# Token-major blocks of 1024 columns, with transposed MLP activations, in a two-layer encoder trunk

## The chip, the cores and the metric

The kernel runs on one core of a Trainium2 chip. What counts is the time of one launch on the device, in microseconds (us); of several runs the median is taken. One further execution of each kernel is recorded by the hardware profiler, and the views of the profile that are read below come from it.

## What is computed

256 tokens of width 2048 go through two layers, in float32. Each layer has a mixer and an MLP, each between two norms. What matters here is the size of the products: the weights of the whole trunk are read once, and everything else is small beside them.

```python
D_MODEL, SEQ, DEPTH, D_FF = 2048, 256, 2, 8192
def reference(x, norm_g, even_w_in, ..., mlp_w1, mlp_w2):
    h = x
    for l in range(DEPTH):
        g = norm_g[l]
        u = rmsnorm(h, g[0])
        if l % 2 == 0:
            proj = u @ even_w_in[e]                      # 2048 x 6144
            b_gate, c_gate, hc, q, k, v = split_cols(proj, EVEN_SIZES)
            ya = short_conv_mixer(b_gate, c_gate, hc, even_conv_w[e])
            yb = chunked_band_attention(q, k, v, even_rel_bias[e])
            y = jnp.concatenate([ya, yb], axis=-1) @ even_w_out[e]     # 2048 x 2048
        else:
            proj = u @ odd_w_in[o_i]                     # 2048 x 7184
            hq, hf, hi, hg, gq, gk, gv, gr, ga = split_cols(proj, ODD_SIZES)
            yc = hgrn2_mixer(hq, hf, hi, hg, lb_all[l], hgrn_norm_g[o_i])
            yd = gla_mixer(gq, gk, gv, gr, ga, gla_wa2[o_i], gla_ba[o_i], gla_norm_g[o_i])
            y = jnp.concatenate([yc, yd], axis=-1) @ odd_w_out[o_i]    # 2048 x 2048
        h = h + rmsnorm(y, g[1])
        u = rmsnorm(h, g[2])
        z = jnp.square(jax.nn.relu(u @ mlp_w1[l])) @ mlp_w2[l]         # 2048 x 8192, 8192 x 2048
        h = h + rmsnorm(z, g[3])
    return h
```

## The kernel before

**Number format.** Each float32 operand is split into a high and a low part of the type fp32r, and each product is made of three: high by high, high by low, low by high.

**Slabs.** Weights come in slabs of 512 KB: one DMA on SyncE's queue into `raw` (3 buffers), a cast on ScalarE to `whi` (L226), and a subtraction on VectorE to `wlo` (L227); `whi` and `wlo` have 8 buffers each, so casts can run ahead of TensorE. There are 784 such loads. Two forms of block use them:

- `Block` is token-major: the activations are the stationary operand, 128 tokens at a time (tile t = 0, then t = 1), and the weights stream by. A slab holds two k-tiles (2 x 128 rows) of 512 columns; for each token tile it gives six matmuls of 512 columns (L240 high by high, L241 by the weights' low part, L242 the activations' low part), 12 a slab. All six add to one PSUM bank (`acc`), which is evacuated after the block's last slab.
- `UpBlock` is feature-major: 128 columns of the weights are stationary, and the activations of all 256 tokens, high and low beside one another, stream by. A slab gives eight pairs of one matmul of 512 columns (L275) and one of 256 (L276), in four banks. The product comes out transposed, as the next product needs it.

Eight PSUM banks are divided: `acc` has `ACC_BUFS` = 3, `aux` has `AUX_BUFS` = 5 (transposes, the small products, and the four banks of the MLP's UpBlocks; `banks()` gives the even mixer two of each).

**Stages.** The even mixer (q, k and the convolution as UpBlock, 80 slabs; v as Block, 16), its output projection `out_proj` (4 Blocks of 8 slabs), the MLP `mlp`, then the odd mixer (112 slabs: `hgrn` twice with f, q, i, g, then `gla` with k, q, r, v, all Block), its `out_proj` and the second MLP. An MLP has 8 chunks of 1024 hidden columns. `up(c)` makes two blocks of 512 columns (8 slabs each), UpBlock but for the very first of each layer, which is a Block whose squares are transposed on TensorE; `down(c-1)` follows `up(c)`, with 4 Blocks of 4 slabs whose results are added into `y` on VectorE (L473). In the odd mixer and the output projection's input, operands that are token-major are turned by `transpose4` (four 128 x 128 transposes on TensorE, L185, into one `aux` bank) and split by `split4` (a copy on ScalarE, a subtraction on VectorE).

**Order.** `run` writes out slabs one after another: load, then the matmuls of both token tiles. With `lead`, the first 6 slabs (`LEAD`) do tile 0 first and tile 1 after; with `tail`, the last 4 slabs (`TAIL`) do so, and `between` puts the norm of tile 0 ahead of the matmuls of tile 1. `later` delays what needs TensorE (transposes) by two slabs; `bg` holds small work of the mixers as generators, a step of which is taken every 1 / `rate` slabs. From this the framework's scheduler sets the order of each engine when the kernel is built, and each engine then runs its own in order.

**Names.** `xt` are the normed activations, `x2` the second product's, `relu`, `relu2`, `ulo` the hidden values on the way. In the odd mixer, `ev_f` turns the forget gate into its logarithm (L871 to L874 on ScalarE), which is then transposed.

```python
            for i in range(SLAB):
                xh, xl = self.lhs(t, self.kts[s * SLAB + i])
                ...
                nc.tensor.matmul(ps, xh, hi[:, i, 0:self.n], start=first, stop=False)
                nc.tensor.matmul(ps, xh, lo[:, i, 0:self.n], start=False, stop=False)
                nc.tensor.matmul(ps, xl, hi[:, i, 0:self.n], start=False, stop=last)
```

## Time and profile before

| what | value |
|---|---|
| runs | 2306.0, 2307.85, 2311.98 us; median 2307.85 |
| span of the profiled execution | 2302.9 us |
| TensorE matmul, busy (PE) | 2276.5 us |
| TensorE weight load, busy (PEld) | 1920.3 us |
| VectorE busy (DVE) | 1412.6 us |
| ScalarE busy (ACT) | 1093.6 us |
| GpSimd busy (POOL) | 15.3 us |
| DMA, mean | 186 GB/s |

The span is that of the program on the core; the runs are launches and lie 3.1 to 9.1 us above it. Times of instructions below are counted from the span's start. A row of the timeline gives start, duration, engine, line and operation, the output and the inputs by their names, and in brackets the idle time ahead of it on its engine and what ended that. A matmul's duration overlaps with that of its neighbours, so that two starts, not one duration, give what it costs.

### The profile page before, as it was taken

What the parts mean: (1) busy time and instruction counts of PE and PEld (TensorE: products, weight loads), DVE (VectorE), ACT (ScalarE), POOL (GpSimd) and SP (SyncE); (2) the same over time, 40 slices, a digit from 0 to 9 for tenths busy, and PEclk for the clock granted to TensorE, in tenths of its full rate; (3) what the DMA queues carried; (4) which work ended last, traced back from release to release, by engine and by line L of the source; (5) the groups of instructions that cost most, each with busy time, mean ns of one, the idle gap of its engine ahead of it and who ended that gap; (6) DMA issues with size and microseconds to landing.
All of it is one profiled execution on the core that took longest, in us unless ns stands there. A gap on an engine that the chain in (4) does not pass through costs nothing.

```text
span 2302.9 us, 30049 instructions
## 1 busy us (share of the span) xinstructions
PE 2276.5 (99%) x11518; PEld 1920.3 (83%) x11518; DVE 1412.6 (61%) x1873; ACT 1093.6 (47%) x1565; POOL 15.3 (1%) x30
## 2 busy tenths in 40 slices
PE   9999999999999999999999999999999999999998
PEld 7888888888888888888788888888888888888886
DVE  6656565755555555555777767657656555555555
ACT  6444445544444444444646454546444444444443
POOL 0000000000000000000000000000000000000000
PEclk9999999999999999999999999999999999999999
DMA  7564665655655556555554544565665655655653
GB/s 242 183 187 150 192 205 172 212 189 192 191 186 190 192 187 189 191 190 193 181 193 156 165 146 156 171 243 167 209 193 189 191 190 186 192 192 185 191 192 119
DMA packets 219231, 428.35 MB, mean 186 GB/s; under 512 B 13362, under 2 KB 14160, under 8 KB 218832
## 3 DMA queue, kind: packets, MB, share of 16 engines
q1 hardware_dynamic: 216992, 420.53, 56.2%
q0 software_dynamic: 1376, 4.79, 0.7%
q8 instruction: 90, 1.47, 0.2%
q10 hardware_dynamic: 720, 1.11, 0.1%
q14 instruction: 53, 0.43, 0.1%
HBM read 422.18 MB, written 4.20 MB: 185 GB/s over the span
## 4 chain that ended last, share of the span: by engine, by line
PE 87%; DMA 5%; DVE 4%; ACT 3%; issue 1%; DVEq 0%; ACTq 0%; POOLq 0%; SPq 0%
PE aux L275 20%; PE acc L240 17%; PE acc L242 17%; PE acc L241 17%; PE aux L276 10%; DMA raw<-e_win 2%; DVE wlo L227 2%; DMA raw<-w 2%; PE acc L275 2%; ACT whi L226 2%; PE aux L796 1%; PE aux L185 1%; PE acc L276 1%; ACT xt L176 1%; ACT junk L359 0%
## 5 line engine op out<-in xcount | busy, mean ns | idle before, releaser
L227 DVE TENSOR_TENSOR wlo<-raw,whi 128x1024 fp32r<-128x1024 f32 x780 | 953.7, 1224 | 785.2 <-ACT whi L226 783.5
L226 ACT CAST whi<-raw 128x1024 fp32r<-128x1024 f32 x780 | 821.5, 1054 | 1038.0 <-PE acc L242 509.8
L275 PE MATMUL aux<-xt,whi 128*128 128x512 f32 x2240 | 798.2, 398 | 1.5 <-DVE relu L453 1.5
L276 PE MATMUL aux<-xt,wlo 128*128 128x256 f32 x2240 | 628.4, 281 | 0.0
L275 PEld LDWEIGHTS aux<-xt,whi 128*128 128x128 f32 x2240 | 421.0, 188 | 105.8 <-DVE relu L453 2.1
L240 PE MATMUL acc<-whi,x 128*128 128x512 f32 x1264 | 493.2, 390 | 1.1 <-DVE relu L476 0.7
L242 PE MATMUL acc<-whi,x 128*128 128x512 f32 x1264 | 492.3, 389 | 0.0
L241 PE MATMUL acc<-wlo,x 128*128 128x512 f32 x1264 | 492.2, 389 | 0.0
L276 PEld LDWEIGHTS aux<-xt,wlo 128*128 128x128 f32 x2240 | 423.1, 189 | 0.5
L240 PEld LDWEIGHTS acc<-whi,x 128*128 128x128 f32 x1264 | 237.3, 188 | 51.0 <-DVE relu L476 1.1
L242 PEld LDWEIGHTS acc<-whi,x 128*128 128x128 f32 x1264 | 237.3, 188 | 49.8
L241 PEld LDWEIGHTS acc<-wlo,x 128*128 128x128 f32 x1264 | 237.3, 188 | 48.7
L240 PE MATMUL acc<-whi,xt 128*128 128x512 f32 x576 | 229.5, 399 | 0.3 <-ACT gate L882 0.3
L241 PE MATMUL acc<-wlo,xt 128*128 128x512 f32 x576 | 226.5, 393 | 0.0
L242 PE MATMUL acc<-whi,xt 128*128 128x512 f32 x576 | 226.0, 393 | 0.0
L242 PEld LDWEIGHTS acc<-whi,xt 128*128 128x128 f32 x576 | 108.7, 189 | 23.2 <-issue 0.3
L240 PEld LDWEIGHTS acc<-whi,xt 128*128 128x128 f32 x576 | 108.8, 189 | 22.4 <-ACT gate L882 0.7
L241 PEld LDWEIGHTS acc<-wlo,xt 128*128 128x128 f32 x576 | 108.9, 189 | 21.4
L275 PE MATMUL acc<-xt,whi 128*128 128x512 f32 x320 | 121.9, 403 | 3.8 <-DVE whole L619 3.8
L276 PE MATMUL acc<-xt,wlo 128*128 128x256 f32 x320 | 90.5, 283 | 0.0
L275 PEld LDWEIGHTS acc<-xt,whi 128*128 128x128 f32 x320 | 60.6, 189 | 18.8 <-DVE whole L619 4.4
L473 DVE TENSOR_TENSOR y<-acc,y 128x512 f32<-128x512 f32 x96 | 61.5, 682 | 0.0
(208 smaller groups left out, 1103.6 us busy)
## 6 DMA issues: line engine op xcount, KB each, us to landing
raw<-w SPq DMA_DIRECT2D x512, 512.0 KB, 3.6
raw<-o_win SPq DMA_DIRECT2D x112, 512.0 KB, 3.7
raw<-e_win SPq DMA_DIRECT2D x96, 512.0 KB, 4.2
raw<-e_wout SPq DMA_DIRECT2D x32, 512.0 KB, 4.3
raw<-o_wout SPq DMA_DIRECT2D x32, 512.0 KB, 3.9
gbc<-norm_g SPq DMA_DIRECT2D x8, 512.0 KB, 6.0
h<-x SPq DMA_DIRECT2D x8, 256.0 KB, 5.4
hsave<-h POOLq DMA_DIRECT2D x2, 1024.0 KB, 4.7
```

The lines of the kernel that those rows point to most:

```text
L176: nc.scalar.activation(out=hi[:, k, :], in_=psv[:, k, :], func=AF.Copy, scale=g[:, k:k + 1])
L185: nc.tensor.transpose(out=ps[:, k * P:(k + 1) * P], in_=src[:, k * P:(k + 1) * P], identity=ident)
L226: nc.scalar.copy(out=hi[:, :, 0:self.n], in_=raw[:, :, 0:self.n])
L227: nc.vector.tensor_tensor(out=lo[:, :, 0:self.n], in0=raw[:, :, 0:self.n], in1=hi[:, :, 0:self.n], op=ALU.subtract)
L240: nc.tensor.matmul(ps, xh, hi[:, i, 0:self.n], start=first, stop=False)
L241: nc.tensor.matmul(ps, xh, lo[:, i, 0:self.n], start=False, stop=False)
L242: nc.tensor.matmul(ps, xl, hi[:, i, 0:self.n], start=False, stop=last)
L275: nc.tensor.matmul(self.ps[j], hi[:, i, cs], x, start=first, stop=False)
L276: nc.tensor.matmul(self.ps[j][:, 0:NT * P], lo[:, i, cs], x[:, 0, :], start=False, stop=last)
L473: nc.vector.tensor_tensor(out=y[t][:, cs], in0=ps, in1=y[t][:, cs], op=ALU.add)
L796: nc.tensor.matmul(ps[0:m, u * 64:(u + 1) * 64].rearrange("p (b n) -> p b n", n=wd), K[:, u * P:u * P + m], Q[:, us].rearrange("p (b two n ...
```

## The change

A third form of block comes in, `Wide`: token-major like Block, but a slab holds one k-tile of 1024 columns, where Block's holds two k-tiles of 512. It is 512 KB as well and gives 12 matmuls of 512 columns too. The two column halves go to two `acc` banks, written in turn, so that one stationary operand serves up to four matmuls after one another. The two halves needn't be neighbours in the weights (`step`). A block has as many slabs as k-tiles, twice as many as a Block over the same rows, and two evacuations for each token tile.

Wide takes the place of Block in both output projections, in the MLP's `down` and in the odd mixer, where f and q, i and g, k and q, the two halves of r and of v are paired; GLA's `decay` now stands ahead of the block for k and q instead of behind that for k. In the MLP, Wide also takes the place of UpBlock in `up`: one block of 16 slabs a chunk. The hidden values then come out token-major: ScalarE takes the ReLU, VectorE the square into `ulo` (now 4 buffers), and two slabs later `transpose4` and `split4` turn them, four sets of four transposes a chunk, into `aux` banks. `acc` gets five banks, `aux` three; the even mixer's UpBlocks, which stay, take three `acc` banks and one `aux`. The even mixer's v stays Block. Of the 784 slabs 688 are now Wide, 80 UpBlock and 16 Block; the loads are as many and as large as before.

```diff
-ACC_BUFS = 3
-AUX_BUFS = 5
+ACC_BUFS = 5
+AUX_BUFS = 3
...
+    class Wide(Block):
+        def __init__(self, wv, n0, n1, kts, lhs, evac):
+            super().__init__(wv, n0, 512, kts, lhs, evac)
+            self.step = n1 - n0
+            self.nslab = len(kts)
+
+        def source(self, s):
+            k = self.kts[s]
+            if self.step == 512:
+                return self.wv[:, k:k + 1, self.n0:self.n0 + 1024].rearrange("p a (b n) -> p (a b) n", n=512)
+            a = self.wv[:, k, self.n0:self.n0 + 512]
+            return bass.AP(tensor=a.tensor, offset=a.offset, ap=[a.ap[0], [self.step, 2], [1, 512]])
+
+        def mm(self, s, t):
+            if s == 0:
+                self.ps[t] = [accp.tile([P, 512], F32, name="acc") for _ in range(2)]
+            ps = self.ps[t]
+            hi, lo = self.w[s]
+            xh, xl = self.lhs(t, self.kts[s])
+            first, last = s == 0, s == self.nslab - 1
+            nc.tensor.matmul(ps[0], xh, hi[:, 0, :], start=first, stop=False)
+            nc.tensor.matmul(ps[1], xh, hi[:, 1, :], start=first, stop=False)
+            nc.tensor.matmul(ps[0], xh, lo[:, 0, :], start=False, stop=False)
+            nc.tensor.matmul(ps[1], xh, lo[:, 1, :], start=False, stop=False)
+            nc.tensor.matmul(ps[0], xl, hi[:, 0, :], start=False, stop=last)
+            nc.tensor.matmul(ps[1], xl, hi[:, 1, :], start=False, stop=last)
+            if last:
+                for j, e in enumerate(self.evac):
+                    e(t, ps[j])
+                del self.ps[t]
...
     def banks():
-        return [accp.tile([P, 512], F32, name="acc") if j % 2 == 0 else aux() for j in range(4)]
+        return [accp.tile([P, 512], F32, name="acc") if j < 3 else aux() for j in range(4)]
...
-        run([Block(wview(w), nb * 512, 512, kts if nb == 0 else ALLK, X2.get, mk(nb)) for nb in range(4)],
-            tail=TAIL, between=between, extra=ypool, hooks=hooks)
+        run([Wide(wview(w), nb * 512, nb * 512 + 512, kts if nb == 0 else ALLK, X2.get, [mk(nb), mk(nb + 1)])
+             for nb in (0, 2)], tail=TAIL, between=between, extra=ypool, hooks=hooks)
...
-                    r2 = ypool.tile([P, 512], F32, name="ulo", bufs=2)
+                    r2 = ypool.tile([P, 512], F32, name="ulo", bufs=4)
                     nc.vector.tensor_tensor(out=r2, in0=r, in1=r, op=ALU.mult)
-                    later(lambda: hid[c].put(t, c * 2 + j, split4(x2p, "x2", transpose4(r2, accp, "acc"))))
+                    later(lambda: hid[c].put(t, c * 2 + j, split4(x2p, "x2", transpose4(r2))))
                 return evac
-            def mk_up(j):
...
-            return [Block(w1v, (c * 2 + j) * 512, 512, ALLK, X.get, mk(j)) if c == 0 and j == 0 else
-                    UpBlock(w1v, (c * 2 + j) * 512, 512, ALLK, X.both, mk_up(j)) for j in range(2)]
+            return [Wide(w1v, c * 1024, c * 1024 + 512, ALLK, X.get, [mk(0), mk(1)])]
...
-            return [Block(w2v, nb * 512, 512, list(range(c * 8, c * 8 + 8)), hid[c].get, mk(nb)) for nb in range(4)]
+            return [Wide(w2v, nb * 512, nb * 512 + 512, list(range(c * 8, c * 8 + 8)), hid[c].get, [mk(nb), mk(nb + 1)])
+                    for nb in (0, 2)]
...
-        return [Block(wv, HF + g * 512, 512, ALLK, X.get, ev_f),
-                Block(wv, HQ + g * 512, 512, ALLK, X.get, ev_q),
-                Block(wv, HI + g * 512, 512, ALLK, X.get, ev_i),
-                Block(wv, HG + g * 512, 512, ALLK, X.get, ev_g)]
+        return [Wide(wv, HF + g * 512, HQ + g * 512, ALLK, X.get, [ev_f, ev_q]),
+                Wide(wv, HI + g * 512, HG + g * 512, ALLK, X.get, [ev_i, ev_g])]
...
-        return ([Block(wv, GK, 512, ALLK, X.get, ev_k)], decay,
-                [Block(wv, GQ, 512, ALLK, X.get, ev_q)] +
-                [Block(wv, GR + i * 512, 512, ALLK, X.get, mk_r(i)) for i in range(2)] +
-                [Block(wv, GV + i * 512, 512, ALLK, X.get, mk_v(i)) for i in range(2)])
+        return decay, [Wide(wv, GK, GQ, ALLK, X.get, [ev_k, ev_q]),
+                       Wide(wv, GR, GR + 512, ALLK, X.get, [mk_r(0), mk_r(1)]),
+                       Wide(wv, GV, GV + 512, ALLK, X.get, [mk_v(0), mk_v(1)])]
...
-    first, decay, rest = gla()
-    run(first, rate=RATE)
+    decay, blocks = gla()
     decay()
-    run(rest, rate=RATE)
+    run(blocks, rate=RATE)
```

How this moves instructions on the engines is shown at the places of which the prediction speaks. Rows give line, operation, output and inputs (names with the number of the buffer) and the shape.

**From up to down in the MLP.** TensorE before: the end of an up block (UpBlock, `aux` banks) and the start of the down blocks:

```order
L275 MATMUL aux_6387<-xt_3501,whi_6538 128x512
L276 MATMUL aux_6387<-xt_3501,wlo_6539 128x256
L240 MATMUL acc_6588<-whi_6584,x2_5643 128x512
L241 MATMUL acc_6588<-wlo_6585,x2_5643 128x512
L242 MATMUL acc_6588<-whi_6584,x2_5643 128x512
L240 MATMUL acc_6588<-whi_6584,x2_5643 128x512
```

The down block takes an `acc` bank that stood idle, and no transposes stand between. TensorE in the changed kernel at the same place, from the last two matmuls of the up block (`acc_5306` and `acc_5307`, the banks of its second token tile) on:

```order
L275 MATMUL acc_5306<-whi_5568,xt_3498 128x512
L276 MATMUL acc_5307<-whi_5568,xt_3498 128x512
L271 MATMUL acc_5606<-whi_5602,x2_4983 128x512
L272 MATMUL acc_5607<-whi_5602,x2_4983 128x512
L273 MATMUL acc_5606<-wlo_5603,x2_4983 128x512
L274 MATMUL acc_5607<-wlo_5603,x2_4983 128x512
L275 MATMUL acc_5606<-whi_5602,x2_4983 128x512
L276 MATMUL acc_5607<-whi_5602,x2_4983 128x512
L271 MATMUL acc_5614<-whi_5602,x2_4999 128x512
L273 MATMUL acc_5614<-wlo_5603,x2_4999 128x512
L272 MATMUL acc_5615<-whi_5602,x2_4999 128x512
L274 MATMUL acc_5615<-wlo_5603,x2_4999 128x512
```

The down block's first slab asks for four banks within twelve matmuls: one stands idle (`acc_5606`), the others are those of the ended block, in the order in which they are read. TensorE in the changed kernel right behind that slab:

```order
L185 MATMUL aux_5622<-ident_82,ulo_5580 128x128 x4
L185 MATMUL aux_5630<-ident_82,ulo_5584 128x128 x4
L185 MATMUL aux_5638<-ident_82,ulo_5594 128x128 x4
L271 MATMUL acc_5606<-whi_5656,x2_4983 128x512
L272 MATMUL acc_5607<-whi_5656,x2_4983 128x512
L273 MATMUL acc_5606<-wlo_5657,x2_4983 128x512
L274 MATMUL acc_5607<-wlo_5657,x2_4983 128x512
L275 MATMUL acc_5606<-whi_5656,x2_4983 128x512
L276 MATMUL acc_5607<-whi_5656,x2_4983 128x512
L271 MATMUL acc_5614<-whi_5656,x2_4999 128x512
L272 MATMUL acc_5615<-whi_5656,x2_4999 128x512
L185 MATMUL aux_5646<-ident_82,ulo_5598 128x128 x4
```

Twelve transposes of the hidden values (`ulo`) now stand behind the down block's first slab, and the last four come eight matmuls later.

ScalarE before, at the end of an up block (the copies of the half products, L449, the casts of weights, L226, and the splits, L458):

```order
L449 COPY ulo_7970<-aux_7808 128x256
L449 COPY ulo_7978<-aux_7809 128x256
L449 COPY ulo_7990<-aux_7810 128x256
L226 CAST whi_8140<-raw_8138 128x1024
L449 COPY ulo_7998<-aux_7811 128x256
L458 CAST x2_7983<-relu2_7981 128x512
L226 CAST whi_8160<-raw_8158 128x1024
L458 CAST x2_8003<-relu2_8001 128x512
```

ScalarE in the changed kernel, around the end of an up block (casts of weights, L229, the four ReLUs, L474, the split, L172):

```order
L229 CAST whi_5746<-raw_5744 128x1024
L474 ACTIVATE relu_5578<-acc_5298 128x512
L474 ACTIVATE relu_5582<-acc_5299 128x512
L229 CAST whi_5764<-raw_5762 128x1024
L474 ACTIVATE relu_5592<-acc_5306 128x512
L474 ACTIVATE relu_5596<-acc_5307 128x512
L229 CAST whi_5786<-raw_5784 128x1024
L172 CAST x2_5627<-aux_5622 128x512
L172 CAST x2_5635<-aux_5630 128x512
```

Four reads of 256 columns, each ahead of VectorE's add, have become four ReLUs of 512 columns, two for each token tile, with a cast of weights between the two pairs.

**The forget gate in the odd mixer.** TensorE before, where the gate's block (`hgrn`, f) has ended and its neighbour has begun:

```order
L240 MATMUL acc_9742<-whi_9792,xt_9372 128x512
L241 MATMUL acc_9742<-wlo_9793,xt_9372 128x512
L242 MATMUL acc_9742<-whi_9792,xt_9372 128x512
L240 MATMUL acc_9742<-whi_9792,xt_9372 128x512
L185 MATMUL aux_9756<-ident_82,v_9708 128x128 x4
L241 MATMUL acc_9742<-wlo_9793,xt_9372 128x512
```

The transposes of the gate (`v_9708`) stand within a slab whose weights are already cast. ScalarE before, at the gate's evacuation (L871) and its logarithm (L873, L874):

```order
L226 CAST whi_9810<-raw_9808 128x1024
L871 ACTIVATE tmp_9709<-acc_9574,nrst_9553 128x512
L226 CAST whi_9828<-raw_9826 128x1024
L873 ACTIVATE tmp_9710<-tmp_9709 128x512
L871 ACTIVATE tmp_9726<-acc_9581,nrst_9557 128x512
L874 ACTIVATE tmp_9710<-tmp_9710 128x512
```

ScalarE in the changed kernel at the end of the paired block of f and q (L889 reads f's bank, L900 q's, L891 and L892 are the logarithm):

```order
L229 CAST whi_9502<-raw_9500 128x1024
L229 CAST whi_9533<-raw_9531 128x1024
L229 CAST whi_9551<-raw_9549 128x1024
L229 CAST whi_9569<-raw_9567 128x1024
L889 ACTIVATE tmp_9345<-acc_9064,nrst_9043 128x512
L900 ACTIVATE gate_9355<-acc_9065,rs_o_8907 128x512
L891 ACTIVATE tmp_9346<-tmp_9345 128x512
L889 ACTIVATE tmp_9357<-gate_9355 128x512
L892 ACTIVATE tmp_9346<-tmp_9346 128x512
```

The gate's evacuation now comes 16 slabs into the mixer instead of 8, behind the cast of slab 22, where the block ends with slab 15; both banks are read there.

**The end of the program.** VectorE before, the last column block of the second token tile and the norm:

```order
L476 TENSOR_TENSOR relu_19203<-acc_19178,y1_12668 128x512
L480 SCALAR_TENSOR_TENSOR y1_12668<-relu_19203,pw2_13548,gbc_13377 128x512
L128 TENSOR_SCALAR rs_v_19208<-ssl_13381,pw4b_13551,based_19102 128x1
L134 SCALAR_TENSOR_TENSOR rs_a_19213<-rs_r_19210,rs_v_19208 128x1
L139 SCALAR_TENSOR_TENSOR rs_o_19215<-rs_a_19213,rs_r_19210 128x1
L579 SCALAR_TENSOR_TENSOR h1_12663<-y1_12668,rs_o_19215,h1_12663 128x256
```

VectorE in the changed kernel:

```order
L493 TENSOR_TENSOR relu_18172<-acc_18003,y1_12158 128x512
L493 TENSOR_TENSOR relu_18183<-acc_18004,y1_12158 128x512
L497 SCALAR_TENSOR_TENSOR y1_12158<-relu_18172,pw2_13039,gbc_12867 128x512
L161 TENSOR_REDUCE rs_t_18177<-ssy_12869 128x1
L497 SCALAR_TENSOR_TENSOR y1_12158<-relu_18183,pw2_13039,gbc_12867 128x512
L155 TENSOR_SCALAR basec_18179<-rs_t_18177,pw4a_13041 128x1
L156 TENSOR_SCALAR based_18180<-basec_18179 128x1
L128 TENSOR_SCALAR rs_v_18188<-ssl_12871,pw4b_13042,based_18180 128x1
L134 SCALAR_TENSOR_TENSOR rs_a_18193<-rs_r_18190,rs_v_18188 128x1
L139 SCALAR_TENSOR_TENSOR rs_o_18195<-rs_a_18193,rs_r_18190 128x1
L597 SCALAR_TENSOR_TENSOR h1_12153<-y1_12158,rs_o_18195,h1_12153 128x256
```

Two column blocks (L493, L497) instead of one stand here, and the sum of the partial squares (L161 to L156) comes between them.

**The start.** TensorE before, in the first slabs, which both programs have as Blocks of the even mixer's v:

```order
L242 MATMUL acc_153<-whi_253,xt_262 128x512
L241 MATMUL acc_160<-wlo_254,xt_262 128x512
L240 MATMUL acc_153<-whi_299,xt_262 128x512
L242 MATMUL acc_160<-whi_253,xt_262 128x512
L240 MATMUL acc_160<-whi_253,xt_262 128x512
L241 MATMUL acc_160<-wlo_254,xt_262 128x512
```

The scheduler mixes the matmuls of the two token tiles, so that two banks are written in turn; in the changed kernel the rows are the same but for the line numbers.

26 lines of the change are left out of this document (6 added, 20 removed).

## The prediction

> **What bounds the kernel now.** I read the page first, then the chain, then the timeline of TensorE at one chunk of the MLP and at every place where it paused.
>
> ```profile
> PE 2276.5 (99%) x11518; PEld 1920.3 (83%) x11518; DVE 1412.6 (61%) x1873; ACT 1093.6 (47%) x1565; POOL 15.3 (1%) x30
> PE 87%; DMA 5%; DVE 4%; ACT 3%; issue 1%; DVEq 0%; ACTq 0%; POOLq 0%; SPq 0%
> ```
>
> TensorE is busy for 99% of the span, and 87% of the chain that ended last is its own. So a time comes out of three things: how many matmuls there are, at what pitch they start, and where TensorE waits. A matmul's duration is not its pitch, since they overlap; pitches are read from starts. One chunk of the MLP in the steady state (16 slabs of UpBlock, then 16 slabs of Block):
>
> ```profile
> 711.28 0.39 PE L275 MATMUL aux<-xt,whi 128*128 128x512 f32 x1
> ...
> 756.50 0.40 PE L240 MATMUL acc<-whi,x 128*128 128x512 f32 x1
> ...
> 800.08 0.39 PE L275 MATMUL aux<-xt,whi 128*128 128x512 f32 x1
> ```
>
> ```profile
> 711.28:756.50 45.22, 45.22 (x258) 39.24 (x257) 24.79 (x28) 19.79 (x25) 0.00 (x0) 1.00 0.57 187
> 756.50:800.08 43.58, 43.58 (x195) 36.03 (x193) 26.73 (x30) 18.55 (x20) 0.00 (x0) 1.00 0.60 193
> ```
>
> In the window rows the columns after the length are busy PE, PEld, DVE, ACT and POOL, then clock, DMA share and GB/s. Both halves do the same multiplications, 16 slabs each, yet the feature-major half takes 45.22 us and the token-major half 43.58 us: 2.826 against 2.724 us a slab, and 43.58 / 192 = 0.227 us a matmul. TensorE never pauses there; VectorE (24.8 of 45.2) and ScalarE (19.8) have room.
>
> **The change, part by part.** *Pitch.* 30 of the MLP's 32 up blocks, 8 slabs each, turn from UpBlock into token-major slabs. 240 slabs x (2.826 - 2.724) = 24.6 us less. This takes the pitch of Block for that of Wide, whose consecutive matmuls write two banks in turn and keep one stationary operand for four. Both occur already: at the start the scheduler mixes the two token tiles, so that from 24.42 on acc_160, acc_153, acc_160 are written one after the other (the rows in the order shown above):
>
> ```profile
> 24.42 0.39 PE L241 MATMUL acc<-wlo,xt 128*128 128x512 f32 x1
> 24.65 0.39 PE L240 MATMUL acc<-whi,xt 128*128 128x512 f32 x1
> 24.88 0.39 PE L242 MATMUL acc<-whi,xt 128*128 128x512 f32 x1
> 25.11 0.39 PE L240 MATMUL acc<-whi,xt 128*128 128x512 f32 x1
> 25.33 0.39 PE L241 MATMUL acc<-wlo,xt 128*128 128x512 f32 x1
> ```
>
> Pitch 0.23, 0.23, 0.23, 0.22: no other than in Block. L240 to L241 keeps the stationary operand, L241 to L242 doesn't, at the same pitch. So I take 0.227 for Wide; the stages that were Block already gain and lose nothing.
>
> *Transposes.* The activations now pass through TensorE: 16 transposes a chunk (twelve, then four in the order), 16 chunks, where two blocks had eight each. Their price is read from two places of the odd mixer:
>
> ```profile
> 1257.71 0.40 PE L242 MATMUL acc<-whi,xt 128*128 128x512 f32 x1
> 1257.94 0.60 PE L185 MATMUL aux<-ident,tmp 128*128 128x128 f32 x4
> 1258.30 0.47 PE L240 MATMUL acc<-whi,xt 128*128 128x512 f32 x1
> ...
> 1259.77 0.40 PE L240 MATMUL acc<-whi,xt 128*128 128x512 f32 x1
> ...
> 1386.80 0.39 PE L242 MATMUL acc<-whi,xt 128*128 128x512 f32 x1
> 1387.03 1.03 PE L185 MATMUL aux<-ident,tmp 128*128 128x128 f32 x8
> ...
> 1389.29 0.39 PE L240 MATMUL acc<-whi,xt 128*128 128x512 f32 x1
> ```
>
> From 1257.71 to 1259.77 are 2.06 us with seven pitches of 0.227 in them, so four transposes add 0.47; from 1386.80 to 1389.29 are 2.49 us, so eight add 0.90. That is 0.108 each and 0.04 for the interruption. Twelve and four: 0.04 + 12 x 0.108 + 0.47 = 1.80 us a chunk, 28.8 for 16, less 2 x 0.90 before: 27.0 us more. Pitch and transposes together: +2.4 us, nearly nothing.
>
> The evacuations: 4 copies and adds of 256 columns a block, then squares and splits, become 2 ReLUs, 2 squares and 2 splits of 512. They go beside TensorE in both programs, and the window rows leave 20 us of VectorE free in each half; I cost them at nothing but for one wait.
>
> *Banks.* A Wide block ends four banks where Block ended two, and five buffers hold accumulators. At the end of an up block ScalarE reads all four, and the order has a cast of weights between the second ReLU and the third. Nearest rows:
>
> ```profile
> L471 ACT COPY y<-acc 128x512 f32<-128x512 f32 x16 | 9.4, 589 | 8.6 <-PE acc L242 8.6
> L226 ACT CAST whi<-raw 128x1024 fp32r<-128x1024 f32 x780 | 821.5, 1054 | 1038.0 <-PE acc L242 509.8 <-PE aux L275 369.9 <-DMA raw<-e_win 43.9
> ```
>
> ```profile
> 2293.53 0.39 PE L242 MATMUL acc<-whi,x 128*128 128x512 f32 x1
> 2293.95 0.69 DVE L476 TENSOR_TENSOR relu<-acc,y 128x512 f32<-128x512 f32 x1
> ```
>
> Count from the first matmul of the last slab's second tile. An engine starts 0.42 us after the start of the matmul it waits for (2293.53 to 2293.95, the last add). First ReLU 0.2 to 0.8, second to 1.4; the cast needs the slab's weights released, 5 x 0.227 + 0.42 = 1.55, to 2.6; third ReLU to 3.2. TensorE wants that bank for its 15th matmul, at 14 x 0.227 = 3.18. The wait is 0.1 us a chunk, 1.6 us in all; bounds 0 and 0.3 x 16 = 4.8. The fourth set of transposes stands eight matmuls behind the third, which lets the first aux bank come free: nothing. At the end of a down block the four evacuations are VectorE's and no cast is between: nothing.
>
> *Start of the odd mixer.* Here is the longest pause of TensorE:
>
> ```profile
> 1143.09 0.39 PE L240 MATMUL acc<-whi,xt 128*128 128x512 f32 x1
> 1148.12 1.09 PE L185 MATMUL aux<-ident,v 128*128 128x128 f32 x4 [4.64 <-issue]
> 1148.86 0.78 PE L241 MATMUL acc<-wlo,xt 128*128 128x512 f32 x1
> ...
> 1152.05 0.39 PE L241 MATMUL acc<-wlo,xt 128*128 128x512 f32 x1
> ```
>
> ```profile
> 1140.95 1.05 ACT L226 CAST whi<-raw 128x1024 fp32r<-128x1024 f32 x1 [4.45 <-DMA raw<-o_win]
> 1141.91 0.63 ACT L873 ACTIVATE tmp<-tmp 128x512 f32<-128x512 f32 x1
> ```
>
> ```profile
> 1148.00:1152.00 4.00, 3.88 (x13) 3.31 (x14) 4.00 (x6) 2.54 (x4) 0.00 (x0) 0.61 0.49 160
> ```
>
> A transpose of the forget gate stands ahead of matmuls whose weights are there; the gate's logarithm (L873) is queued on ScalarE behind a cast that waited 4.45 us for a load. Afterwards the granted clock is 0.61 for 4 us. From 1143.09 to 1152.05 are 8.96 us for ten pitches (2.27) and one set (0.47): 6.2 us lost. With Wide the gate is evacuated after 16 slabs, not 8, and no transpose stands there any more. But what is late next is the same: in the changed order the first evacuation of the f and q block stands behind the cast ten slabs after the one that was late. A load lands in 3.7 us:
>
> ```profile
> raw<-o_win SPq DMA_DIRECT2D x112, 512.0 KB, 3.7
> ```
>
> With cast (1.05) and subtraction (1.2) one of three raw buffers turns round in 6.0 us. Slabs 12 to 14 are late together, slab 15 is cast 6.0 us after 1140.95, slab 21 at 1159, slab 22 at 1160 to 1161; the gate's first operation ends at about 1161.7. TensorE, without the pause, ends slab 15's first tile at 1157.4 and wants that bank at 1159. So some 3 us of the 6.2 come back: -3.2, bounds -6.2 and 0.
>
> *Ends of stages.* In a tail two column blocks are evacuated where one was. After the last matmul (2293.53, above):
>
> ```profile
> 2294.68 0.63 ACT L479 ACTIVATE junk<-relu 128x512 f32<-128x512 f32 x1 [4.00 <-DVE relu L476]
> 2294.68 0.75 DVE L480 SCALAR_TENSOR_TENSOR y<-relu,pw,gbc 128x512 f32<-128x512 f32 x1
> 2296.54 2.87 DVE L579 SCALAR_TENSOR_TENSOR h<-y,rs_o,h 128x256 f32<-128x256 f32 x5
> ```
>
> The order puts one more add (0.65 behind another) and one more product (0.75) on VectorE ahead of the three small operations that the norm needs: 0.65 + 0.75 + some 0.3 = 1.7 us, uncovered (bounds 1.4 and 2.0). The two output projections and the first MLP have such tails too, where four slabs of the second tile, 24 x 0.227 = 5.4 us, cover the first's norm, and slabs of the next stage cover the second's. Bounds: 0, and 1.7 each, 5.1; I take half, 2.5.
>
> SyncE issues as many loads of the same size, POOL's queue is unchanged; out of the odd mixer two more head groups are finished beside the output projection, whose first 8 slabs (21.8 us) don't need them: nothing.
>
> Sum: -24.6 + 27.0 + 1.6 - 3.2 + 1.7 + 2.5 = +5.0 us, on a span of 2302.9; the median of the runs, 2307.85, stands 4.95 above it, taken as constant. 2307.85 + 5.0 = 2312.9 us.
>
> **Rivals.** *Slower: a second cast ahead of the third ReLU.* If ScalarE is later than counted by a whole cast, each up block waits 1.05 us more: 16.8, 2330 us. It decides as soon as the third ReLU ends after 3.2 us. For it speaks that my margin is nothing; against it, that the next cast needs a slab which TensorE has not read then.
>
> *Slower: late weights at every block of the odd mixer.* If the stock of cast slabs stays short, each of its seven Wide blocks waits the 3 us worked out for one: 18 more, 2331 us. ScalarE's waits for these loads speak for it (18 of them, 38.0 us together):
>
> ```profile
> ACT whi L226 <- DMA raw<-o_win: 38.0, 18, 5.9
> ```
>
> Against it speaks the room between 6.0 / 3 = 2.0 us a load and 2.72 us a slab.
>
> *Faster: bank alternation shortens the pitch.* If writing one bank without pause is what costs the time, all 688 Wide slabs gain. Any nanosecond is worth 688 x 12 = 8.3 us, so 1 ns decides. The rows at 24.42 speak against it: four steps in 0.91 us are 0.2275. Their smallest step, 0.22, would be 0.007 x 8256 = 58 us less, 2255 us. The Trainium skill (TensorE: Matmul & The Clock Gate, Back-to-back issue gap) gives N / 2.4 + 2.5 ns for a matmul by itself, 216 ns for 512 columns; Block's 0.227 differs from it, and the measurement decides; by it the estimate would be 0.011 x 8256 = 91 us less, 2222 us.
>
> *Slower: a transpose costs its duration.* The group's row:
>
> ```profile
> L185 PE MATMUL aux<-ident,tmp 128*128 128x128 f32 x40 | 6.3, 275 | 0.1
> ```
>
> At 0.275 us each 240 more are 66 us, not 27.0: 2352 us. The starts, 0.108 apart, speak against it. The Trainium skill (the same page, PE-mode transpose) has about 275 ns in a kernel too; the trace agrees with that as a duration, not as a pitch.
>
> **How the numbers follow.** About 0.3%, 6.9 us, is what a measurement of this kernel can tell from no change. My forecast's own bounds: -24.6 + 27.0 + 0 - 6.2 + 1.4 + 0 = -2.4 and -24.6 + 27.0 + 4.8 + 0 + 2.0 + 5.1 = +14.3, that is 2305 to 2322. It gets 0.60: 0.45 of it within 6.9 us, 0.15 above. The second cast gets 0.15, late weights 0.10 (0.08 slower, 0.02 partly and within), the shorter pitch 0.12, the dear transposes 0.03. Faster 0.12, same 0.45 + 0.02 = 0.47, slower 0.15 + 0.15 + 0.08 + 0.03 = 0.41. The range, 2300 to 2333, takes in the second cast and the late weights, and at its lower end half a nanosecond of pitch (4 us) under the forecast's bound; it leaves out the pitch at its full price and the dear transposes, 0.15 together.
>
> **What would show it.** An up chunk of 16 slabs at 45.4 us (43.6 + 1.8) beside a down half still at 43.6; L185 in the MLP 0.108 apart; pauses of TensorE under 0.3 us where acc passes from up to down; no pause at the forget gate's transposes but one at the first matmuls behind the f and q block; some 11 us from the last matmul to the end, against 9.4. A pitch other than 0.227 in Wide would make all this wrong, and so would a pause at each chunk.

## The result and the profile after

The changed kernel takes 2334.85 us (median of 4 runs, 2332.64 to 2343.4) beside 2307.26 us before: a ratio of 1.0124, 95% interval 1.011 to 1.0137. That is 27.6 us slower, where 5 were forecast, and 2 us above the range. The first lines of the page, busy time and the chain, of the changed kernel:

```profile
PE 2292.3 (98%) x10798; PEld 1897.1 (81%) x10798; DVE 1371.1 (59%) x1753; ACT 1086.1 (47%) x1505; POOL 15.2 (1%) x30
PE 81%; DMA 8%; DVE 5%; ACT 5%; issue 1%; ACTq 0%; DVEq 0%; SPq 0%; POOLq 0%
```

TensorE's share of the chain fell from 87 to 81%, and loads, VectorE and ScalarE took its place: TensorE waits more. In the steady chunks it doesn't compute more slowly. One chunk of the MLP, the up half and then the down half, in the window rows:

```profile
719.00:762.63 43.63, 43.63 (x194) 35.96 (x192) 21.90 (x21) 17.97 (x18) 0.00 (x0) 1.00 0.61 195
762.63:808.24 45.61, 45.61 (x210) 37.47 (x209) 26.81 (x29) 19.89 (x22) 0.00 (x0) 1.00 0.58 183
```

The pair was 45.22 + 43.58 = 88.80 us and is 89.24. The up half became 1.6 us shorter by its pitch, and the down half holds the transposes. So the steady MLP gives 0.44 us a chunk, about 5 us in twelve chunks, and the rest is elsewhere. The table goes by stages: each row is the difference between the starts of the first block matmuls of two neighbouring stages, read from the timeline of TensorE; "end" is from the last matmul to the end of the span. "First ups" are up(0) and up(1) of a layer, "steady" its down(0) to up(7), "last downs" down(6) and down(7). The columns after the difference are experiments, told below. Each column is one profiled execution. The steady rows repeat within 0.4 us from kernel to kernel where their form and banks are the same, but the even mixer, which is the same in several of the kernels, moves by up to 3 us, so differences of that size in a row that waits for loads are not firm. The spans differ by 31.1 us where the medians differ by 27.6.

| us | before | changed | more | tails as Block | six acc banks | 6/7 buffers | before, 6/7 buffers |
|---|---|---|---|---|---|---|---|
| start and even mixer | 307.3 | 307.4 | 0.1 | 307.1 | 307.9 | 299.3 | 297.9 |
| output projection 0 | 90.1 | 90.6 | 0.6 | 89.0 | 89.4 | 89.0 | 89.6 |
| first ups 0 | 92.8 | 97.1 | 4.3 | 94.3 | 93.9 | 93.3 | 91.9 |
| steady 0 | 532.7 | 535.3 | 2.6 | 535.3 | 533.5 | 535.7 | 532.7 |
| last downs 0 | 90.5 | 93.1 | 2.6 | 90.9 | 92.2 | 92.8 | 89.5 |
| odd mixer | 375.5 | 375.3 | -0.2 | 371.2 | 374.9 | 369.5 | 368.9 |
| output projection 1 | 92.7 | 101.0 | 8.3 | 96.8 | 99.9 | 96.6 | 92.7 |
| first ups 1 | 92.3 | 97.0 | 4.7 | 95.3 | 94.2 | 93.4 | 92.1 |
| steady 1 | 532.7 | 535.4 | 2.6 | 535.3 | 533.5 | 535.4 | 532.7 |
| last downs 1 | 86.9 | 89.8 | 2.9 | 88.9 | 89.4 | 89.2 | 86.9 |
| end | 9.4 | 12.1 | 2.7 | 9.4 | 12.1 | 12.0 | 9.4 |
| span | 2302.9 | 2334.1 | 31.1 | 2313.5 | 2320.9 | 2306.2 | 2284.3 |

Three places carry most of it: the start of each MLP (9.0), the second output projection (8.3), and the last downs with the end (8.2, of which 3.6 are the transposes of two chunks). In the second output projection TensorE idles 2.9 us instead of 0.1, and 48 of its matmuls are small work instead of 32. Here is the pause between the first two up blocks, TensorE in the timeline:

```profile
443.89 0.39 PE L271 MATMUL acc<-whi,xt 128*128 128x512 f32 x1
446.94 0.79 PE L272 MATMUL acc<-whi,xt 128*128 128x512 f32 x1 [2.67 <-ACT relu L474]
447.54 0.63 PE L273 MATMUL acc<-wlo,xt 128*128 128x512 f32 x1
```

```profile
446.94:453.00 6.06, 6.06 (x17) 4.89 (x18) 4.31 (x6) 3.43 (x6) 0.00 (x0) 0.50 0.76 238
```

In the window row, the 6 us behind the pause run at a granted clock of 0.50, and matmuls start 0.43 us apart. ScalarE at the same time:

```profile
442.99 1.05 ACT L229 CAST whi<-raw 128x1024 fp32r<-128x1024 f32 x1 [0.96 <-DMA raw<-w]
445.35 1.04 ACT L229 CAST whi<-raw 128x1024 fp32r<-128x1024 f32 x1 [1.32 <-DVE wlo L230]
446.30 1.08 ACT L474 ACTIVATE relu<-acc 128x512 f32<-128x512 f32 x2
447.74 1.05 ACT L229 CAST whi<-raw 128x1024 fp32r<-128x1024 f32 x1 [0.36 <-DVE wlo L230]
```

The new block writes its first matmul into the one idle bank and needs a bank of the ended block for the second. The ReLU that frees it stands on ScalarE behind the cast of the slab seven further on (the order of the engine), and that cast is late: the casts come 2.0 and 2.4 us apart, after waits for a load and for the subtraction of the slab before. TensorE has four or five cast slabs in stock here (counted by the ends of the subtractions), after the lead-in has used them up. In the steady chunks, with six or seven, the same order costs 0.3 us, since that cast is done in time. The odd mixer has the same picture, the load named outright:

```profile
1170.12:1176.48 6.36, 0.38 (x2) 0.00 (x0) 3.43 (x4) 3.28 (x5) 0.00 (x0) 0.75 0.77 226
1176.48:1180.06 3.58, 3.58 (x8) 2.81 (x9) 2.24 (x5) 3.12 (x6) 0.00 (x0) 0.50 0.80 245
```

```profile
1152.29 1.05 ACT L229 CAST whi<-raw 128x1024 fp32r<-128x1024 f32 x1 [3.04 <-DMA raw<-o_win]
...
1174.80 1.04 ACT L229 CAST whi<-raw 128x1024 fp32r<-128x1024 f32 x1 [1.66 <-DMA raw<-o_win]
1175.75 0.68 ACT L889 ACTIVATE tmp<-acc,nrst 128x512 f32<-128x512 f32 x1
```

For 6.36 us TensorE does one matmul, and then eight in 3.58 us at a granted clock of 0.50. And here is the end of the MLP before it, where the second tile's last matmul starts at 1119.91:

```profile
1119.91 0.39 PE L276 MATMUL acc<-whi,x 128*128 128x512 f32 x1
1122.36 1.29 PE L185 MATMUL aux<-ident,h 128*128 128x128 f32 x8 [2.06 <-DVE h L415]
```

```profile
1114.67 1.29 DVE L493 TENSOR_TENSOR relu<-acc,y 128x512 f32<-128x512 f32 x2 [1.48 <-PE acc L275]
1118.93 1.23 DVE L230 TENSOR_TENSOR wlo<-raw,whi 128x1024 fp32r<-128x1024 f32 x1 [0.88 <-ACT whi L229]
1120.20 0.69 DVE L493 TENSOR_TENSOR relu<-acc,y 128x512 f32<-128x512 f32 x1
1121.47 2.73 DVE L415 SCALAR_TENSOR_TENSOR h<-y,rs_o,h 128x512 f32<-128x512 f32 x4
```

From the first tile's evacuation (1114.67) to the transposes of its normed activations (1122.36) are 7.7 us. Besides the second column block, the subtraction of a slab (1118.93) and the second tile's own adds (1120.20) stand in that chain. The second tile's 24 matmuls cover 5.4. In the kernel before, the same chain took 3.6 us, VectorE and then TensorE, and the transposes came while the second tile still had matmuls left:

```profile
1105.71 0.69 DVE L476 TENSOR_TENSOR relu<-acc,y 128x512 f32<-128x512 f32 x1 [1.51 <-PE acc L242]
```

```profile
1109.26 0.63 PE L185 MATMUL aux<-ident,h 128*128 128x128 f32 x4 [0.19 <-DVE h L379]
```

At the very end the second tile's add waits for VectorE, which is still adding the first tile's result to `h`:

```profile
2320.82 2.87 DVE L597 SCALAR_TENSOR_TENSOR h<-y,rs_o,h 128x256 f32<-128x256 f32 x5
2322.00 0.39 PE L276 MATMUL acc<-whi,x 128*128 128x512 f32 x1
2323.60 1.28 DVE L493 TENSOR_TENSOR relu<-acc,y 128x512 f32<-128x512 f32 x2
```

It starts 1.6 us after the start of the last matmul; in the kernel before it was 0.42.

### The profile page after: what moved, and what is told of

Same layout as the page of the kernel before. It is cut to its first block, busy times and chain, and to the rows that moved or that the text cites. A ratio compares the mean times of both kernels' runs of the same rounds, so it can differ in the third digit from the quotient of the medians.

```text
span 2334.1 us, 28358 instructions
## 1 busy us (share of the span) xinstructions
PE 2292.3 (98%) x10798; PEld 1897.1 (81%) x10798; DVE 1371.1 (59%) x1753; ACT 1086.1 (47%) x1505; POOL 15.2 (1%) x30
## 4 chain that ended last, share of the span: by engine, by line
PE 81%; DMA 8%; DVE 5%; ACT 5%; issue 1%; ACTq 0%; DVEq 0%; SPq 0%; POOLq 0%
PE acc L272 12%; PE acc L274 12%; PE acc L276 12%; PE acc L275 12%; PE acc L271 12%; PE acc L273 12%; PE acc L311 3%; DVE wlo L230 3%; ACT whi L229 2%; DMA raw<-e_win 2%; DMA raw<-w 2%; DMA raw<-o_win 2%; PE aux L185 2%; PE acc L312 1%; DMA raw<-o_wout 1%
## 5 line engine op out<-in xcount | busy, mean ns | idle before, releaser
L229 ACT CAST whi<-raw 128x1024 fp32r<-128x1024 f32 x780 | 822.8, 1055 | 1118.9 <-PE acc L276 826.4
L272 PE MATMUL acc<-whi,xt 128*128 128x512 f32 x736 | 290.7, 395 | 12.7 <-ACT relu L474 6.5
L271 PE MATMUL acc<-whi,xt 128*128 128x512 f32 x736 | 290.8, 395 | 0.0
L273 PE MATMUL acc<-wlo,xt 128*128 128x512 f32 x736 | 288.1, 391 | 0.0
L276 PE MATMUL acc<-whi,xt 128*128 128x512 f32 x736 | 287.9, 391 | 0.0
L274 PE MATMUL acc<-wlo,xt 128*128 128x512 f32 x736 | 287.8, 391 | 0.0
L275 PE MATMUL acc<-whi,xt 128*128 128x512 f32 x736 | 287.8, 391 | 0.0
L311 PE MATMUL acc<-xt,whi 128*128 128x512 f32 x480 | 174.3, 400 | 3.6 <-DVE whole L637 3.6
L272 PEld LDWEIGHTS acc<-whi,xt 128*128 128x128 f32 x736 | 138.8, 189 | 44.4 <-ACT relu L474 7.8
L275 PEld LDWEIGHTS acc<-whi,xt 128*128 128x128 f32 x736 | 138.8, 189 | 29.3
L276 PEld LDWEIGHTS acc<-whi,xt 128*128 128x128 f32 x736 | 138.7, 188 | 29.1
L274 PEld LDWEIGHTS acc<-wlo,xt 128*128 128x128 f32 x736 | 138.8, 189 | 28.6
L273 PEld LDWEIGHTS acc<-wlo,xt 128*128 128x128 f32 x736 | 138.9, 189 | 28.2
L271 PEld LDWEIGHTS acc<-whi,xt 128*128 128x128 f32 x736 | 138.7, 188 | 28.0 <-ACT whi L229 0.2
L272 PEld LDWEIGHTS acc<-whi,x 128*128 128x128 f32 x632 | 118.9, 188 | 34.8 <-DVE y L490 3.6
```

The lines of the kernel that those rows point to most:

```text
L229: nc.scalar.copy(out=hi[:, :, 0:self.n], in_=raw[:, :, 0:self.n])
L271: nc.tensor.matmul(ps[0], xh, hi[:, 0, :], start=first, stop=False)
L272: nc.tensor.matmul(ps[1], xh, hi[:, 1, :], start=first, stop=False)
L273: nc.tensor.matmul(ps[0], xh, lo[:, 0, :], start=False, stop=False)
L274: nc.tensor.matmul(ps[1], xh, lo[:, 1, :], start=False, stop=False)
L275: nc.tensor.matmul(ps[0], xl, hi[:, 0, :], start=False, stop=last)
```

## Experiments

Times are medians; the runs of the kernel before beside them had medians of 2308.0, 2310.0, 2311.0 and 2309.0 us in the four groups.

**Fewer weight buffers.** `-W_BUFS = 8` `+W_BUFS = 5` in the changed kernel.

> The changed kernel with W_BUFS = 5 instead of 8, nothing else. Theory A (late evacuation): the 27 us come mostly from pauses of TensorE at ends of Wide blocks, where ScalarE reads the banks only after the cast of the slab seven further on (the order has it there because 8 buffers allow it), and that cast waits for a load. With 5 buffers the cast ahead of the read is that of the slab four on. The pauses at 308, 444, 1170, 1551 and 1646 us (1.6 + 3.1 + 6.4 + 2.5 + 4.3, and some 3 us of lower clock behind them) go, except 2 to 4 us: 2312 to 2322 us, and no pause over 1.5 us at the up-to-up boundaries. Theory B (the form itself: transposes and token-major products are dear, the pauses only shift): the same 2335 us within 3, or slower, since fewer buffers leave less stock of cast slabs.

Measured: 2325.47 us, between the two theories. The pauses at 444 and 1646 are gone, and the order shows why: the ReLU now stands behind the cast of the slab four on. But the first ups took 96.3 and 94.8 us, since with less stock TensorE waits in the lead-in instead, and the odd mixer took 375.3 us as it did: its one pause of 6.4 us had become three, of 3.5, 1.4 and 1.3. There the late cast is where the shortage shows, not what makes it. Of the 13.2 us less in the span, 5.8 came in the even mixer, which I hadn't expected.

**Six banks for accumulators.** `-ACC_BUFS = 5` `+ACC_BUFS = 6`, `-AUX_BUFS = 3` `+AUX_BUFS = 2`.

> The changed kernel with six acc banks and two aux banks instead of five and three. Theory A: the next block now has two idle banks, so TensorE asks for a bank of the ended block six matmuls (1.36 us) later; each of the five long pauses shortens by 1.0 to 1.4 us, and the transposes wait a little for the two aux banks: 2327 to 2333 us. If the late cast were of no account and the number of banks all, the pauses would shrink to under 1 us: 2318. Theory B: 2335 within 3, or slower by the aux banks.

Measured: 2322.63 us, between A's range and the 2318 us of the case that the number of banks is all. First ups 3.2 and 2.8 us shorter; the pause at the odd mixer 4.8 us instead of 6.4. The steady chunks show the wait for banks by itself:

```profile
714.46:757.98 43.52, 43.52 (x193) 36.04 (x192) 21.90 (x21) 17.96 (x18) 0.00 (x0) 1.00 0.62 194
757.98:803.37 45.39, 45.39 (x210) 37.64 (x208) 26.87 (x29) 19.89 (x22) 0.00 (x0) 1.00 0.58 184
```

88.91 us a chunk, 0.33 less than with five, and 45.39 - 43.58 = 1.81 us for the transposes, against the 1.80 predicted.

**UpBlock in up.** The changed kernel with

```diff
-            return [Wide(w1v, c * 1024, c * 1024 + 512, ALLK, X.get, [mk(0), mk(1)])]
+            return [Block(w1v, (c * 2 + j) * 512, 512, ALLK, X.get, mk(j)) if c == 0 and j == 0 else
+                    UpBlock(w1v, (c * 2 + j) * 512, 512, ALLK, X.both, mk_up(j), banks) for j in range(2)]
```

> The changed kernel with the MLP's up blocks as in the kernel before (UpBlock, but for the first block of each MLP), in three acc banks and one aux. Theory A: 27 us of transposes go and 24.6 us of pitch come back, the two up-to-up pauses with their lower clock (about 10 us) and the quarter microsecond a chunk (4 us) go: 2316 to 2322 us; the odd mixer and the output projections keep their pauses. Theory B (transposes dear): 2307 to 2312 us, nearly everything is back.

Measured: 2320.23 us, as A said. So some 12 us of the 27.6 remain when the MLP's up has its old form.

**Block in the odd mixer.** `-Wide(wv, HF + g * 512, HQ + g * 512, ...)` and the other four to `+Block(wv, HF + g * 512, 512, ALLK, X.get, ev_f)` and so on, as before.

> The changed kernel with the odd mixer's blocks as in the kernel before (Block, 512 columns). Theory A: the pause of 6.4 us at the forget gate becomes the old one of 5.0 or less, since the idle acc bank lets the first products go on, and the small work that had moved behind the odd mixer, with the waits beside it, comes back: odd mixer and its output projection together 3 to 7 us shorter, 2328 to 2332 us. Theory B: the odd mixer has the same products either way: 2335 within 2.

Measured: 2330.93 us, as A said; odd mixer and output projection together 469.0 us instead of 476.3 (468.3 before). The pause shrank as A said, from 6.0 us idle to 3.4 and 1.4, but the odd mixer took 376.1 us, no less than the 375.3. The whole gain is in the second output projection, which is back at 92.8.

**Supply.** `-RAW_BUFS = 3` `+RAW_BUFS = 7` and `-W_BUFS = 8` `+W_BUFS = 6`, the same memory, in the changed kernel (first text) and in the kernel before (second).

> The changed kernel with W_BUFS = 6 and RAW_BUFS = 7 instead of 8 and 3 (the same memory). Theory A1 (the supply of slabs is held by the turnaround of three raw buffers; the pauses at block ends come where the stock is short): with seven raw buffers loads run ahead through the lead-ins, the stock stays at five or more, and the pauses at 308, 444, 1170, 1551 and 1646 us nearly go: 2310 to 2317 us, with casts at the odd mixer's start less than 2.0 us apart instead of 2.25. Theory A2 (the DMA's rate is the bound there): casts stay 2.2 us apart, only the order of the reads helps as with W_BUFS = 5: 2322 to 2327 us.

> The kernel before with W_BUFS = 6 and RAW_BUFS = 7. Theory A1: its pause of 5.0 us at 1143 with the lower clock behind it (6.2 us), and those of 2.1 and 2.3 us in the even mixer, go for the most part: 2296 to 2302 us, and the difference to the changed kernel with the same buffers is the form's own price, about 13 to 16 us (bank waits, later small work, end). Theory A2: 2305 to 2309 us.

Measured: 2308.86 us and 2286.3 us (ratio to the kernel before 0.9901, 0.9887 to 0.9916: the fastest of all kernels run here). Both gained more than A1 said. ScalarE's waits for the odd mixer's loads were 38.0 us before. In the changed kernel, and then, as the only waits for weights of over 1 us in all, in the one with seven raw buffers:

```profile
ACT whi L229 <- DMA raw<-o_win: 82.6, 40, 4.6
```

```profile
ACT whi L229 <- DMA raw<-e_win: 2.2, 4, 0.8
ACT whi L229 <- DMA raw<-o_wout: 1.7, 1, 1.7
```

No wait for `o_win` is left. ScalarE in the odd mixer with seven raw buffers:

```profile
1131.47 3.02 ACT L229 CAST whi<-raw 128x1024 fp32r<-128x1024 f32 x3
...
1137.74 1.05 ACT L229 CAST whi<-raw 128x1024 fp32r<-128x1024 f32 x1 [1.66 <-PE acc L276]
1140.46 1.05 ACT L229 CAST whi<-raw 128x1024 fp32r<-128x1024 f32 x1 [1.67 <-PE acc L276]
```

Three casts follow one another at once, and from then on they come 2.72 us apart, a slab's time on TensorE, and wait for TensorE to give back a weight buffer. So the DMA's rate (A2) was not the bound. That five weight buffers alone gave 9.4 us leaves open how much of the gain is due to six weight buffers and how much to seven raw ones: each number was not tried by itself. The difference between the two kernels is 22.6 us, not the 13 to 16 that I expected: the shortage of slabs costs the changed kernel 26.0 us and the kernel before 21 to 24, and most of the change's price stands without it.

**Other pairs in GLA.** `-Wide(wv, GR, GR + 512, ..., [mk_r(0), mk_r(1)])`, `+Wide(wv, GV, GR, ALLK, X.get, [mk_v(0), mk_r(0)])`, and the second halves likewise.

> The changed kernel with GLA's last two Wide blocks paired otherwise: v's first half with r's first, v's second with r's second, instead of r with r and v with v. The first head pair can then be finished 16 slabs before the odd mixer ends. Theory A (the 8.3 us more in the odd mixer's output projection come of the small work that starts 16 slabs later and runs into it, delaying ScalarE and VectorE at the block boundary): that stage goes from 101.0 to 95 or 97 us, the odd mixer itself stays or grows by at most 3: 2329 to 2333 us. Rival (the stage is slow by itself, since Wide has two banks to evacuate with ScalarE's squares): 101 us stay, 2335.

Measured: 2332.2 us; the second output projection 94.2 us instead of 101.0, the odd mixer 378.4, 3.1 more. As A said, the late small work costs; on balance of the two stages it is 3.7 us. The medians differ by 2.7, and the runs of the two kernels overlap.

**Tails as Block.** Both output projections and the last down:

```diff
-        run([Wide(wview(w), nb * 512, nb * 512 + 512, kts if nb == 0 else ALLK, X2.get, [mk(nb), mk(nb + 1)])
-             for nb in (0, 2)], tail=TAIL, between=between, extra=ypool, hooks=hooks)
+        run([Block(wview(w), nb * 512, 512, kts if nb == 0 else ALLK, X2.get, mk(nb)) for nb in range(4)],
+            tail=TAIL, between=between, extra=ypool, hooks=hooks)
...
+            if c == NCH - 1:
+                return [Block(w2v, nb * 512, 512, list(range(c * 8, c * 8 + 8)), hid[c].get, mk(nb)) for nb in range(4)]
```

> The changed kernel with Block in both output projections and in the last down of each MLP, that is wherever a stage ends in a tail. Theory A: from the last matmul to the end 9.4 us instead of 12.1, the pauses of 1.6 and 2.5 us in the output projections' middle go: 7 to 9 us less, 2326 to 2329 us. Rival (the tails cost nothing but at the very end): 2332 us.

Measured: 2317.81 us, 17.0 less, and 20.5 in the span: twice the 7 to 9 us of A, and far more than the rival's 3. At the same transition:

```profile
1112.55 0.39 PE L245 MATMUL acc<-whi,x 128*128 128x512 f32 x1
1113.12 0.30 PE L185 MATMUL aux<-ident,h 128*128 128x128 f32 x1 [0.18 <-DVE h L415]
```

The pause went from 2.06 to 0.18 us, the end from 12.1 to 9.4, the pauses in the middle of the output projections are gone, and by the table the gain spreads into the stages that follow: 2.8 and 1.7 us in the first ups, 4.1 in the odd mixer, 4.2 in the second output projection.

**Wide in the tails alone.** The kernel before with the three edits of the last experiment the other way round, five acc and three aux banks, and UpBlocks in three acc and one aux; and the control with these banks and no Wide.

> The kernel before with Wide only where a stage ends in a tail (both output projections and the last down of each MLP); to make room, five acc and three aux banks, and the MLP's UpBlocks in three acc and one aux. Theory T (the tail is the cause: the second token tile's norm comes 1 to 2 us later, TensorE has done the next stage's lead-in by then, weight buffers stay held and the stock for the next stage is shorter): 12 to 18 us over the control, with a pause of about 2.4 us at the transposes of each lead-in and 12 us from the last matmul to the end. Rival (the tail matters only where Wide also stands behind it and asks for four banks): 4 to 7 us over the control.

> The control for it: the kernel before with five acc and three aux banks, UpBlocks in three acc and one aux, and no Wide at all. Both theories: within 4 us of the kernel before, 2305 to 2312.

Measured: 2315.75 and 2304.84 us, 10.9 apart, between the two expectations. By stages: output projections 1.7 and 0.6, first ups 0.5 and 0.4, last downs 2.2 and 0.4, odd mixer 2.5, end 2.6, together 10.9. This leaves the even mixer out, where the two programs do the same and the profiled executions differ by 3.3 us the other way; the spans lie 7.6 apart. At the lead-in of the odd mixer TensorE waits as in the changed kernel:

```profile
1114.04 1.25 PE L185 MATMUL aux<-ident,h 128*128 128x128 f32 x6 [1.97 <-DVE h L415]
```

**Tails as Block and 6/7 buffers**, in the changed kernel.

> The changed kernel with Block in the tails, and 6 weight and 7 raw buffers. Theory T: beside the kernel before with the same buffers (2286.3) there stay transposes less pitch (2.4), bank waits of the steady chunks (4.5), up-to-up (2 to 3) and the late small work in the second output projection (4): 2297 to 2301 us. Rival (the tails only shift a shortage of slabs, which the seven raw buffers have already removed): 2305 to 2309 us, as without Block in the tails.

Measured: 2299.47 us, as T said, 13.2 over the kernel before with the same buffers. The sum fits better than its parts: the first ups gave 0.4 and 0.3 us, not the 2 to 3 of T.

**All that helped, without the tails.** 6/7 buffers, six acc banks, v paired with r.

> The changed kernel with all that took something off it: 6 weight and 7 raw buffers, six acc and two aux banks, v paired with r. Theory A (what the change costs beside pitch and transposes is the waits for banks, the late small work and the tails): against the 2308.9 us of 6 and 7 buffers the bank waits of the steady chunks (14 x 0.35 = 4.9), some of the up-to-up pauses (2) and most of the 3.9 us in the second output projection go: 2296 to 2302 us; over the kernel before with the same buffers (2286.3) there stay the end (2.6), transposes less pitch (2.4) and the lead-ins (5). Theory B (these waits hide one another): 2305 to 2310 us.

Measured: 2306.93 us, as B said. The steady chunks gained 4.1 us (533.5 twice), the second output projection 5.0. But the odd mixer grew by 4.4 us (the small work is now in it), the even mixer by 1.6, and the first ups by 1.3 each. That the two aux banks cause this last part was not tried by itself.

**Runs of 2 KB.** `-rawp.tile([P, SLAB, 512], ...)` `+rawp.tile([P, SLAB, 520], ...)`.

> The changed kernel with a raw buffer whose two halves lie 32 bytes apart, so that a load is moved in runs of 2 KB as in the kernel before, not of 4 KB. The time to landing of an MLP load went from 3.6 to 4.2 us with the change. Theory A (that is waiting behind other loads, not the runs): 4.2 us and 2335 us stay, within 3. Rival (runs of 4 KB land later and starve the casts): 3.6 us come back, the pauses shrink, 2320 to 2330 us.

Measured: 2376.99 us; both were wrong. Landing fell to 3.9 us, but the time didn't. What moved was TensorE's pitch, which belongs to the last section with these three:

> The changed kernel with 192 bytes per partition between the raw and the weight buffers: whi and wlo lie 192 bytes further on (from 320 to 0 modulo 512), exactly as in the run with the gap inside the raw buffer; loads and raw buffers are as they were. Theory P (the place of the streamed weights sets the pitch of the matmuls): pitch 0.233 instead of 0.227 and some 2377 us again. Rival R (the gap in the raw buffer, that is runs of 2 KB and a cast that reads over the gap, slows TensorE's reads): pitch 0.227 and 2335 us.

> The kernel before with 6 weight and 7 raw buffers (2286.3 us), and 192 bytes ahead of all buffers, so that activations, raw and cast weights all lie at 0 modulo 512 instead of 320. If the place of the streamed operand alone counts (0 slow, 320 fast): token-major matmuls 0.233, some 2305 us or more. If the place of the two operands relative to one another counts: 0.227 and 2286 us, as before. If the gap in the raw buffer was the cause: 2286 us too.

> The kernel before with 6 weight and 7 raw buffers (2286.3 us) and 256 bytes between raw and weight buffers, so that cast weights lie 256 bytes on from the activations modulo 512. If the pitch follows the distance modulo 512 and 192 was slow by being no multiple of 256: 0.227 and 2286 us. If any distance but zero is slow: 0.233 for token-major matmuls, 2305 to 2325 us. If a distance can also be better than zero: under 2280 us.

Measured: 2372.73 us, as P said; 2288.15, as if the place of the two operands relative to one another counts; and 2286.49, as the first of its three said.

## Why the prediction was wrong

The forecast had the MLP's arithmetic right and the joints wrong. For new pauses, neither its terms nor its rivals' prices held the lower clock that follows, though it had read such a clock, 0.61, behind the old one.

- *Pitch* (-24.6) held. Wide runs at 0.227 us a matmul, and alternating banks give nothing; the rival of a shorter pitch fell, and so did that of dear transposes.
- *Transposes* (+27.0) held: 1.81 us a chunk against 1.80. The sign named for them put them into the up half; by the order shown above they stand behind the down block's first slab, and it is the down half that grew.
- *Banks* (+1.6) failed in two ways. In the steady chunks six banks took off 1.8 and 1.9 us in the layers' six chunks each, 0.31 a chunk, the upper bound that I gave (0.3) and not the 0.1 that I took. And it was counted only where up passes to down. The boundary from up(0) to up(1) comes right behind the lead-in, with few slabs in stock; there TensorE idles 2.7 and 3.9 us, with the clock of 0.50 behind it, and six banks took off 6.0 us in the two layers. It is the "second cast" rival's mechanism in a milder form: a cast ahead of the reading, once a layer, where it is late, not at every block.
- *Start of the odd mixer* (-3.2) failed: -0.2. I let a cast slab come every 2.0 us; the ten casts up to 1174.80 came 2.25 us apart (from 1152.29). With Block in the tails the stage does become shorter by 4.3 us than before, so the gain is there, and the tail ahead of it took it back (the pause at the gate is then 3.6 us idle, not 6.0). That the two head groups "finished beside the output projection" cost nothing was wrong as well: that stage is 8.3 us longer, of which better pairs took off 6.8 and gave 3.1 back in the mixer.
- *Ends of stages* (+1.7 and +2.5) is the step that failed most. I took the second tile's 5.4 us of matmuls for cover of the first tile's norm, and added 1.7 us at most to the norm's chain. It grew by 4.1, from 3.6 to 7.7 us: the second column block, casts and subtractions of weights and the second tile's own adds stand in it. So TensorE waits 2 us there, and the stages behind it lose time as well. They begin with less in stock: at the end of each lead-in of six slabs two further slabs are cast and split, where the kernel before and the run with Block in the tails have three (counted by the ends of the subtractions). With Wide in the tails alone there are two as well, with six banks three, so the count is a coarse one. At the very end the add also had to wait for the first tile's residual on VectorE: 12.1 us, 2.7 more than before and not 1.7. Both terms together stood at 4.2 us; the tails cost 10.9 us when put into the kernel before, and gave 17.0 when taken out of the changed one.
- *Late weights* as a rival fell in the form given (3 us at each block of the odd mixer: there is one long pause, the other boundaries show 0.6 us or less), and was right in direction. The run with 6 and 7 buffers shows that the shortage is old: the kernel before gains 21 to 24 us by them as well.

The 4.95 us that the forecast put between span and median moves no term, but it is not a constant of the kernel: each launch of the changed kernel lies 2.0 to 3.1 us above its own span.

The parts don't add up without rest: tails (17), banks (6 and 3.6 by the stages) and small work (4) are more than the 27.6 less the 2.4 of pitch and transposes; an explanation that fits is that each shortens the stock that the next one needs. With tails and supply taken out 13.2 us stay. The stages give of it 5.2 in the steady chunks, 4.0 in the second output projection, 3.4 in the last downs (where the transposes of two chunks are 3.6). Of the 4.0 hardly any is waiting: TensorE idles 0.4 us in that stage instead of 0.1, but has 48 small matmuls instead of 32. The odd mixer, with 16 small ones less, took 1.4 us less in return.

## What to carry to other kernels

A form of block that is equal in its steady state is to be costed at its joints: how many banks end at once, what stands ahead of their evacuation on its engine, and whether the work beside the last tile still covers the norm ahead of the next stage. A cover is a length of time and must be compared with the whole chain that it hides, with what the scheduler puts between, not with the operations that are added. And where a pause is put down to a load, try more buffers at the loading end first: here 6 and 7 instead of 8 and 3, in the same memory, gave more than any change of form (21 to 26 us, against 17 for the tails).

## What the runs showed of the hardware

The pitch of a token-major matmul depends on how the streamed weights lie relative to the activations. 192 bytes more ahead of the weight buffers, nothing else changed, made a down half of 192 matmuls and 16 transposes 46.62 us instead of 45.61, and the up half behind it 44.80 us instead of 43.63:

```profile
679.68:726.30 46.62, 46.62 (x209) 37.35 (x208) 26.80 (x29) 19.79 (x22) 0.00 (x0) 1.00 0.58 180
726.30:771.10 44.80, 44.80 (x193) 35.83 (x192) 21.91 (x21) 17.84 (x18) 0.00 (x0) 1.00 0.60 188
```

So a matmul went from 0.227 to 0.233 us, at a granted clock of 1.00. In the built program, by its addresses, which no trace shows, both operands lie at 320 modulo 512 bytes in a partition; with the weights at 0 and the activations at 320 it is slow, with both at 0 (192 bytes ahead of all) and with the weights 256 bytes on it is not: there a down half of 192 matmuls took 43.56 us in both runs. So distances of 0 and 256 are fast and 192 is slow. Other distances were not tried, and the two fast ones were moved in the kernel before, the slow one in the changed kernel. The run with the gap in the raw buffer moved the weights by the same 192 bytes, and its time, 2376.99 us beside 2372.73, needs no other cause than that, its runs of 2 KB least of all. The Trainium skill (SBUF — State Buffer, Who interferes with whom) gives TensorE two read ports, for the moving operand and for the weight load, that are independent; these runs show that the time of the two together does depend on where they lie. Why it does so is open.
